# Transposes of 128 by 128 blocks in two row halves with 64 by 64 identities

## The chip, the cores and the metric

The kernel runs on one core of one Trainium2 chip. The metric is the device time of one execution in microseconds. TensorE multiplies matrices, VectorE and ScalarE work elementwise, GpSimd does small copies, and SyncE issues the DMAs.

## The reference

One layer of a hybrid decoder runs on 256 prompt tokens and 8 tokens of 8 sequences that are being decoded, 264 columns in all, everything in fp32:

```
h = rms_norm(x, g_pre_mix);  z = h @ w_in              # q, k, v, u
attn = sliding-window attention (window 128, 16 heads of 64, 2 kv heads, ALiBi, sinks)
ssm  = 64 groups of 16 channels, complex diagonal state of 64:
       s_t = ab * s_{t-1} + bb u_t ;  y = Re(C s) + D u ;  gelu ; per-group GLU
x += rms_norm([rms_norm(attn); rms_norm(ssm)] @ w_out)
x += rms_norm(SwiGLU(rms_norm(x)))                     # d_ff 5632
x += sigmoid(x @ w_ple_gate) * (p @ w_ple_proj)
```

The outputs are both x, the last 128 keys and values, and the last states.

## The kernel before

Activations lie transposed, with the model dimension on the 128 partitions and the 264 tokens as columns. The weights come from DRAM as 367 blocks of 512 KB in a fixed order (`UNITS`): `in`, `oa`, `os`, `pp`, `gu`, `dn`, `pg`. From the fifteenth block on each is split into a high and a low part, by ScalarE (`wh`) and VectorE (`wl`), and every 128 by 128 block makes three products of 264 columns into an accumulator `acc`: high with high, high with low, low with high.

The first stage does `in` and `oa`, and beside it all of the attention and of the state-space model. `os` needs the whole result of the latter, and from there on weight products follow one another to the end. Inside the first stage the state-space model runs in eight rounds e. `ssm_x` builds a table X on VectorE, transposes it on TensorE in eight blocks (tile `px`, line 968, copied to `XT`), makes `ph` in column tiles of 32, transposes that once (`ht`) and sends it through DRAM to get the table T. `ssm_w` multiplies the inputs with XT and T (`pw`, `py`), copies `pw` to `ws` and transposes it in four blocks (`pw2`, line 1049) to `wt`, on which VectorE runs the scan. `ssm_y` adds the state's part to `py` in 64 by 64 products (line 1112), applies GELU, transposes in four blocks (`py2`, line 1123) to `yt`, and stores that for `ssm_glu`, which loads it as `gt`. The attention runs in eight groups g; each transposes its probabilities in six blocks (`pt`, lines 586 to 589) to `ptt`, which the products `o` use. The profile names tiles without their numbers: `pw2` shows as pw and `py2` as py on line 289.

A transpose is one TensorE instruction, `PE.transpose(out, in_, ident)`: the block is the stationary operand, and a 128 by 128 identity moves through. Products whose operands lie on 64 of the 128 rows or go to 64 or 32 of the 128 columns are made in tiles of the array: `s` (64 rows), `o`, `pw` and `py` with T (64 columns), the state's part of `py` (64 by 64), `ph` (32 columns).

The program's order is not written out by hand. Each piece of work is a generator that names the engine it needs next and what it waits for; `Pace.run` keeps a modelled clock for each engine with a cost per instruction (`tr`: 0.11 us) and takes the piece that can start first, and by a priority among equals. Accumulator banks are counted there: 8 in all, 3 kept for weight products (`acc`, 2 after the tenth block) and the others (`bk`) for everything else; `"+bk:2"` asks for two. The scheduler under it places instructions once more in the first stage; from `os` on the order stays as written.

Of the kernel before, what the change touches and what calls it, by code (L numbers as in the profile page):

```python
# [16 lines left out]
P = 128  # L17
# [180 lines left out]
def build(nc, tc, ctx, a):  # L198
    pace = Pace()
    V, S, G, PE, SP = nc.vector, nc.scalar, nc.gpsimd, nc.tensor, nc.sync  # L200
# [86 lines left out]
    def tr(out, in_, ident):  # L287
        pace.use("pe", 0.11)
        PE.transpose(out, in_, ident)  # L289

    def dma(out, in_):
        n = 4.0
# [24 lines left out]
    def bank(shape, name):  # L317
        return banks.tile(shape, F32, tag="bank", name=name)
# [5 lines left out]
    ident = const.tile([P, P], F32, name="ident")  # L324
# [219 lines left out]
    def attn(g):  # L544

        yield "pe", [f"q{g}", "k", "v", "c_at"] + ([f"sfree{g - 1}"] if g else []) + ["+bk:2"]
        q = qt.pop(g)

        sh = [bank([P, 384], f"s{h}") for h in range(2)]
        for c, b, n in ((0, 0, 128), (128, 128, 256)):  # L550
            for h in range(2):
                r = slice(64 * h, 64 * h + 64)
                mm(sh[h][:, c:c + n], q[r, b:b + 128], kt[r, 0:n], 0.115 if n == 128 else 0.22)
        pace.rel("q")
        yield "dve"
        s = ph1.tile([P, 768], F32, tag="s", bufs=1, name="s")
        mx = ph1.tile([P, 4], F32, tag="mx", bufs=2, name="mx")
        nm = ph1.tile([P, 4], F32, tag="nm", bufs=2, name="nm")
        es = ph1.tile([P, 4], F32, tag="es", bufs=2, name="es")
        den = ph1.tile([P, 4], F32, tag="den", bufs=2, name="den")  # L560
        for i, (dst, src, dd) in enumerate((
                (s[:, 0:128], sh[0][:, 0:128], dist[:, 128:256]), (s[:, 128:256], sh[1][:, 0:128], dist[:, 128:256]),
                (s[:, 256:512], sh[0][:, 128:384], dist), (s[:, 512:768], sh[1][:, 128:384], dist))):
            pace.use("dve", 0.13 + 1.042e-3 * size(dst))
            V.tensor_tensor_reduce(out=dst, in0=src, in1=dd, scale=-slopes[(i % 2) * GRP + g],
                                   scalar=sinks[:, g, i:i + 1], op0=ALU.add, op1=ALU.max, accum_out=mx[:, i:i + 1])
        pace.rel("bk", 2)
        ts(nm, mx, -1.0, ALU.mult)
        sub(es, sinks[:, g, :], mx)
        yield "act"  # L570
        act(es, es, ACTF.Exp)
        offs = [(0, 128), (128, 256), (256, 512), (512, 768)]
        for i, (b, e) in enumerate(offs):
            act(s[:, b:e], s[:, b:e], ACTF.Exp, bias=nm[:, i:i + 1], accum_out=den[:, i:i + 1])
        yield "dve"
        add(den, den, es)
        pace.use("dve", 0.1)
        V.reciprocal(out=den, in_=den)
        yield "act"
        for i, (b, e) in enumerate(offs):  # L580
            act(s[:, b:e], s[:, b:e], scale=den[:, i:i + 1])
        yield "pe", "+bk:2"
        pts = []
        for h in range(2):
            pt = bank([P, 3, P], "pt")
            tr(pt[:, 0, :], s[:, 128 * h:128 * h + 128], ident)
            for b in range(2):
                o = 256 + 256 * h + 128 * b
                tr(pt[:, 1 + b, :], s[:, o:o + 128], ident)
            pts.append(pt)  # L590
        pace.sig(f"sfree{g}", "pe")
        yield "act", "+ptt"
        ptt = ph1.tile([P, 2, 3, P], F32, tag="ptt", bufs=1, name="ptt")
        for h in range(2):
            act(ptt[:, h], pts[h])
        pace.rel("bk", 2)
        yield "pe", "+bk"
        o = bank([P, 256], "o")
        for h in range(2):
            r = slice(64 * h, 64 * h + 64)  # L600
            mm(o[r, :], vnat[:, 0, r], ptt[:, h, 0:2, :], 0.24, stop=False)
        for h in range(2):
            r = slice(64 * h, 64 * h + 64)
            mm(o[r, 128:256], vnat[:, 1, r], ptt[:, h, 2, :], 0.14, start=False)
        pace.rel("ptt")
        yield "act", ["+sqa", "ah"]
        ah = AH["t"]
        sq = ph1.tile([P, 256], F32, tag="sqa", bufs=1, name="sqa")
        act(ah[:, g, 0:256], o, scale=gat[:, g:g + 1])
        act(sq, o, ACTF.Square)  # L610
        yield "dve"
        stt(ah[:, 8 + g, 0:256], o, gat[:, g:g + 1], r32(ah[:, g, 0:256]), ALU.mult, ALU.subtract)
        pace.rel("bk")
        pace.rel("sqa")
        if g == 0:
            pace.use("dve", 0.2)
            V.tensor_copy(out=ssq_a[:, 0:256], in_=sq)
        else:
            add(ssq_a[:, 0:256], ssq_a[:, 0:256], sq)
        pace.sig(f"at{g}", "dve")  # L620
# [329 lines left out]
    def ssm_x(e):  # L950
        yield "sp", ["+X", "+xt", "iss4"]
        xtab = ph1.tile([P, 512], F32, tag="xtab", name="xtab")
        dma(xtab, a["xtab"][e])
        b = xtab[:, 0:128].rearrange("p (r g c) -> p r g c", r=2, g=4)
        cb = xtab[:, 128:384].rearrange("p (r g c) -> p r g c", r=2, g=4)
        dp = xtab[:, 384:512]
        bs = ph1.tile([P, 4, 16], F32, tag="bs", name="bs")
        yield "pool"
        padd(bs, b[:, 0], b[:, 1])
        pcopy(cb[:, 1], cb[:, 1], -1.0)  # L960
        yield "dve", ["tab", "+sc"]
        X = ph1.tile([P, 2, 4, 8, 16], F32, tag="X", name="X")
        yield from outer(X, al_re, al2, b, bs, e)
        yield "pe", ["+bk:3", "+ht"] + ([f"Wpe{e - 1}"] if e else [])
        px = [bank([P, 4, P], f"px{i}") for i in range(2)]
        for g in range(4):
            for ri in range(2):
                tr(px[ri][:, g, :], X[:, ri, g].rearrange("p j c -> p (j c)"), ident)
        ph = bank([P, P], "ph")
        for g in range(4):  # L970
            for ri in range(2):
                PE.matmul(ph[32 * g:32 * g + 32, :], cb[:, ri, g, :], X[:, ri, g].rearrange("p j c -> p (j c)"),
                          start=(ri == 0), stop=(ri == 1), tile_position=(0, 32 * g))
                pace.use("pe", 0.11)
        pace.rel("X")
        yield "act"
        xt = ph1.tile([P, 4, 2, 2, 64], F32, tag="XT", bufs=1, name="XT")
        XT[e] = xt
        ht = ph1.tile([P, P], F32, tag="ht", name="ht")
        act(ht, ph)  # L980
        for ri in range(2):
            act(xt[:, :, :, ri, :], px[ri].rearrange("p g (h q) -> p g h q", h=2))
        pace.rel("bk", 3)
        pace.sig(f"XT{e}", "act")
        yield "pe", "+bk"
        p2 = bank([P, P], "p2")
        tr(p2, ht, ident)
        pace.rel("ht")
        yield "dve"
        t7 = ph1.tile([P, P], F32, tag="t7", name="t7")  # L990
        add(t7, p2, dp)
        pace.rel("bk")
        yield "sp", [f"U{e - NT2}"] if e >= NT2 else ["c_zero"]

        d = td[e % 2][:]
        dma(td[e % 2][0:P], t7)
        pace.rel("xt")
        yield "sp"
        dma(T2[e % NT2], bass.AP(tensor=d.tensor, offset=d.offset, ap=[[P, P], [16 * P, 8], [1, P]]))
        pace.sig(f"T{e}", "sp")  # L1000
# [14 lines left out]
    def ssm_w(e):  # L1015
        q, hf = e // 2, e % 2
# [3 lines left out]
        for h in range(2):  # L1020
            c = q + 4 * h
# [3 lines left out]
        xt = XT.pop(e)  # L1025
# [10 lines left out]
        for g in range(4):  # L1036
            for h in range(2):
                o = 16 * (2 * g + h)
                r = 64 * (h ^ (g % 2))
# [3 lines left out]
        ws = ph1.tile([P, 4, P], F32, tag="ws", bufs=1, name="ws")  # L1043
        act(ws, pw)
        pace.rel("bk")
        yield "pe", "+bk"
        p2 = bank([P, 4, P], "pw2")
        for g in range(4):
            tr(p2[:, g, :], ws[:, g, :], ident)
        pace.rel("ws")  # L1050
        yield "act", ["+wt", "as0"]
        wt = ph1.tile([P, 2, 4, 41], F32, tag="wt", name="wt")
        for h in range(2):
            for ri in range(2):
                act(wt[64 * h:64 * h + 64, ri], p2[64 * ri:64 * ri + 64, :, 64 * h:64 * h + 41])
        pace.rel("bk")
        yield "dve", [f"rho{e}", "rot2"]
        C2, S2 = ct[:, gsl(e), :].unsqueeze(1).to_broadcast([P, 2, 4, 32]), st2[:, :, gsl(e), :]
        t1, t2, sh = rt1, rt2, rsh
# [41 lines left out]
    def ssm_y(e):  # L1101
        q, hf = e // 2, e % 2
# [14 lines left out]
        for i in range(2):  # L1117
            act(gy[:, i::2, :], py[i], ACTF.Gelu_apprx_tanh)
        pace.rel("bk", 2)
        yield "pe", "+bk"  # L1120
        p2 = bank([P, 4, P], "py2")
        for g in range(4):
            tr(p2[:, g, :], gy[:, g, :], ident)
        pace.rel("ws")
        yield "act", "+yt"
        yt = ph1.tile([P, 4, P], F32, tag="yt", name="yt")
        act(yt[:, 0::2, :], p2[:, 0::2, :])
        act(yt[:, 1::2, :].rearrange("p g (h k) -> p g h k", h=2), p2[:, 1::2, :].rearrange("p g (h k) -> p g h k", h=2)[:, :, ::-1, :])
        pace.rel("bk")
        yield "sp"  # L1130
        dma(ys[q].rearrange("r c g h k -> (r c) g (h k)")[:, gs, :], yt)
        pace.sig(f"ys{q}{hf}", "sp")
# [610 lines left out]
```

## Time and profile before

| | |
|---|---|
| median of 3 runs | 1196.16 us (1195.06 to 1196.48) |
| profiled execution | 1194.09 us |
| its span, first to last instruction | 1192.3 us |
| TensorE products | 1172.4 us busy, 98% |
| VectorE | 744.7 us, 62% |
| ScalarE | 577.1 us, 48% |
| granted TensorE clock | 0.999 |

Products are pipelined, and the end of each in the profile is modelled: a product of 264 columns shows as 0.28 us though the next starts 0.12 us later. So distances between starts tell what an instruction costs, not its shown duration.

### The profile page before, as it was taken

The page shows a single profiled execution, that of the slowest core. Times are in us where ns is not written, and L with a number is a line of the kernel's source. Part 1 is how long each engine was busy: PE and PEld are TensorE (multiplying, and loading weights), DVE is VectorE, ACT ScalarE, POOL GpSimd, SP SyncE. Part 2 cuts the span into 40 slices and gives each one's busy share as a digit, 9 for nine tenths or more (in the row PEclk, how much of TensorE's full clock was granted, in tenths as well). Part 3 has the DMA queues.
Part 4 walks back from the last instruction along what each step waited for, and adds up shares of the span by engine and source line. Part 5 has one row for each costly group of instructions (what it writes and reads, how often), then busy time and mean ns, then how long its engine had stood idle before and what let it go on. Part 6 is the DMA issues. An engine that isn't in the chain of part 4 may idle for free.

```text
span 1192.3 us, 24043 instructions
## 1 busy us (share of the span) xinstructions
PE 1172.4 (98%) x9785; PEld 1142.1 (96%) x9785; DVE 744.7 (62%) x1316; ACT 577.1 (48%) x917; POOL 57.5 (5%) x96
## 2 busy tenths in 40 slices
PE   9999999989999999999999999999999999999998
PEld 7789888879999999999999999999999999999998
DVE  8888889857896555555555555555444444446864
ACT  6267886444655444444444444444333443345542
POOL 4113122100000000000000000000000000000000
PEclk9999999999999999999999999999999999999999
DMA  7866655656676565555555566556755555556683
GB/s 269 256 206 187 178 162 172 199 180 200 211 252 178 182 186 181 184 183 179 182 182 184 178 181 188 180 180 199 242 178 179 181 185 180 179 181 216 202 250 111
DMA packets 102053, 228.95 MB, mean 192 GB/s; under 512 B 26711, under 2 KB 50359, under 8 KB 101431
## 3 DMA queue, kind: packets, MB, share of 16 engines
q1 hardware_dynamic: 101943, 227.43, 60.7%
q8 instruction: 76, 1.25, 0.4%
q14 instruction: 34, 0.28, 0.1%
HBM read 214.60 MB, written 12.80 MB: 191 GB/s over the span
## 4 chain that ended last, share of the span: by engine, by line
PE 85%; DVE 8%; DMA 3%; ACT 2%; issue 1%; SPq 0%; POOL 0%; ACTq 0%; DVEq 0%; POOLq 0%
PE acc L285 80%; DVE wl L222 1%; PE py L285 1%; DMA T<-td 1%; DVE rt L222 1%; DMA pt<-in_p 1%; ACT s L281 1%; DMA xr<-in_x 0%; DVE xl L222 0%; DVE sc L222 0%; DVE ssq_x L222 0%; PE px L289 0%; DVE X L222 0%; SPq L296 0%; DMA gt<-ys 0%
## 5 line engine op out<-in xcount | busy, mean ns | idle before, releaser
L222 DVE TENSOR_TENSOR wl<-raw,wh 128x1024 fp32r<-128x1024 f32 x354 | 432.7, 1223 | 305.6 <-PE acc L285 278.7
L281 ACT ACTIVATE wh<-raw 128x1024 fp32r<-128x1024 f32 x354 | 375.5, 1061 | 439.5 <-PE acc L285 428.2
L285 PE MATMUL acc<-hh,wh 128*128 128x264 f32 x1408 | 399.5, 284 | 0.0
L285 PE MATMUL acc<-hl,wh 128*128 128x264 f32 x1408 | 398.3, 283 | 0.5 <-DVE hl L236 0.5
L285 PE MATMUL acc<-hh,wl 128*128 128x264 f32 x1408 | 398.6, 283 | 0.0
L285 PEld LDWEIGHTS acc<-hl,wh 128*128 128x128 f32 x1408 | 265.0, 188 | 0.8 <-DVE hl L236 0.7
L285 PEld LDWEIGHTS acc<-hh,wh 128*128 128x128 f32 x1408 | 265.2, 188 | 0.0
L285 PEld LDWEIGHTS acc<-hh,wl 128*128 128x128 f32 x1408 | 264.0, 188 | 0.0
L285 PE MATMUL acc<-f,wh 128*128 128x264 f32 x1408 | 256.8, 284 | 0.0
L285 PEld LDWEIGHTS acc<-f,wh 128*128 128x128 f32 x1408 | 217.8, 188 | 0.1
L285 PE MATMUL acc<-f,wl 128*128 128x264 f32 x704 | 199.7, 284 | 0.0
L285 PEld LDWEIGHTS acc<-f,wl 128*128 128x128 f32 x704 | 132.5, 188 | 0.0
L285 PE MATMUL acc<-x2h,wh 128*128 128x264 f32 x256 | 72.7, 285 | 0.0
L285 PE MATMUL acc<-x2h,wl 128*128 128x264 f32 x256 | 72.5, 284 | 0.0
L285 PE MATMUL acc<-x2l,wh 128*128 128x264 f32 x256 | 71.9, 284 | 0.2 <-DVE x2l L222 0.2
L285 PE MATMUL acc<-xh,wh 128*128 128x264 f32 x176 | 54.2, 308 | 0.0
L285 PE MATMUL acc<-xt,raw 128*128 128x264 f32 x224 | 52.1, 390 | 1.7 <-ACT xt L281 1.7
L285 PEld LDWEIGHTS acc<-xt,raw 128*128 128x128 f32 x224 | 42.3, 192 | 10.1 <-ACT xt L281 2.6
L222 DVE TENSOR_TENSOR uu<-acc,Rf 128x264 f32<-128x264 f32 x44 | 19.0, 432 | 51.0 <-PE acc L285 51.0
L285 PE MATMUL acc<-xh,wl 128*128 128x264 f32 x176 | 50.3, 286 | 0.0
L285 PE MATMUL acc<-xl,wh 128*128 128x264 f32 x176 | 50.1, 285 | 0.0
L285 PE MATMUL acc<-aops,wh 128*128 128x264 f32 x256 | 50.0, 293 | 0.0
(323 smaller groups left out, 1335.3 us busy)
## 6 DMA issues: line engine op xcount, KB each, us to landing
raw<-in_w SPq DMA_DIRECT2D x367, 512.0 KB, 3.6
T<-td SPq DMA_DIRECT2D x8, 512.0 KB, 4.8
xs<-in_x SPq DMA_DIRECT2D x2, 1056.0 KB, 6.9
ppd<-ppt SPq DMA_DIRECT2D x16, 132.0 KB, 3.6
x1d<-oo SPq DMA_DIRECT2D x4, 528.0 KB, 4.6
x<-x1d SPq DMA_DIRECT2D x2, 1056.0 KB, 8.9
ppr<-ppd SPq DMA_DIRECT2D x16, 132.0 KB, 3.9
xtab<-in_xtab SPq DMA_DIRECT2D x8, 256.0 KB, 3.4
```

Source lines behind the costliest of these rows:

```text
L222: V.tensor_tensor(out=out, in0=in0, in1=in1, op=op)
L281: S.activation(out=out, in_=in_, func=func, **kw)
L285: PE.matmul(out, lhsT, rhs, start=start, stop=stop)
```

## The change

A new helper `trh` makes a transpose in two instructions. Half h takes rows 64h to 64h+63 of the block as stationary operand (64 rows, 128 columns) and the 64 by 64 identity on the same rows as the moving one; its result is 64 columns wide. The two halves go to two different tiles, each in a bank of its own, so px and pt are divided between their two banks by row half instead of by part, and `pw2` and `py2` take two banks in place of one. The copies out of the banks follow: those of px and pt keep number and size, those of `wt` too, and `yt` is made in four copies of 128 columns in place of two of 256. Four places use it: the six transposes of `pt`, eight of `px`, four of `pw2`, four of `py2`. Those of `ht`, of v and of the decode tokens' attention stay. The planner's cost is 0.056 us for a half.

```diff
--- before.py
+++ after.py
@@ -287,6 +287,13 @@
     def tr(out, in_, ident):
         pace.use("pe", 0.11)
         PE.transpose(out, in_, ident)
+
+    def trh(outs, in_):
+
+        for h, out in enumerate(outs):
+            r = slice(64 * h, 64 * h + 64)
+            pace.use("pe", 0.056)
+            PE.transpose(out, in_[r], ident[r, r])
 
     def dma(out, in_):
         n = 4.0
@@ -580,19 +587,17 @@
         for i, (b, e) in enumerate(offs):
             act(s[:, b:e], s[:, b:e], scale=den[:, i:i + 1])
         yield "pe", "+bk:2"
-        pts = []
+        pts = [bank([P, 2, 3, 64], f"pt{i}") for i in range(2)]
         for h in range(2):
-            pt = bank([P, 3, P], "pt")
-            tr(pt[:, 0, :], s[:, 128 * h:128 * h + 128], ident)
+            trh([pt[:, h, 0, :] for pt in pts], s[:, 128 * h:128 * h + 128])
             for b in range(2):
                 o = 256 + 256 * h + 128 * b
-                tr(pt[:, 1 + b, :], s[:, o:o + 128], ident)
-            pts.append(pt)
+                trh([pt[:, h, 1 + b, :] for pt in pts], s[:, o:o + 128])
         pace.sig(f"sfree{g}", "pe")
         yield "act", "+ptt"
         ptt = ph1.tile([P, 2, 3, P], F32, tag="ptt", bufs=1, name="ptt")
-        for h in range(2):
-            act(ptt[:, h], pts[h])
+        for i in range(2):
+            act(ptt[:, :, :, 64 * i:64 * i + 64], pts[i])
         pace.rel("bk", 2)
         yield "pe", "+bk"
         o = bank([P, 256], "o")
@@ -965,7 +970,7 @@
         px = [bank([P, 4, P], f"px{i}") for i in range(2)]
         for g in range(4):
             for ri in range(2):
-                tr(px[ri][:, g, :], X[:, ri, g].rearrange("p j c -> p (j c)"), ident)
+                trh([px[h][:, g, 64 * ri:64 * ri + 64] for h in range(2)], X[:, ri, g].rearrange("p j c -> p (j c)"))
         ph = bank([P, P], "ph")
         for g in range(4):
             for ri in range(2):
@@ -978,8 +983,8 @@
         XT[e] = xt
         ht = ph1.tile([P, P], F32, tag="ht", name="ht")
         act(ht, ph)
-        for ri in range(2):
-            act(xt[:, :, :, ri, :], px[ri].rearrange("p g (h q) -> p g h q", h=2))
+        for h in range(2):
+            act(xt[:, :, h], px[h].rearrange("p g (r q) -> p g r q", r=2))
         pace.rel("bk", 3)
         pace.sig(f"XT{e}", "act")
         yield "pe", "+bk"
@@ -1043,17 +1048,17 @@
         ws = ph1.tile([P, 4, P], F32, tag="ws", bufs=1, name="ws")
         act(ws, pw)
         pace.rel("bk")
-        yield "pe", "+bk"
-        p2 = bank([P, 4, P], "pw2")
+        yield "pe", "+bk:2"
+        p2 = [bank([P, 4, 64], f"pw2{h}") for h in range(2)]
         for g in range(4):
-            tr(p2[:, g, :], ws[:, g, :], ident)
+            trh([p2[h][:, g, :] for h in range(2)], ws[:, g, :])
         pace.rel("ws")
         yield "act", ["+wt", "as0"]
         wt = ph1.tile([P, 2, 4, 41], F32, tag="wt", name="wt")
         for h in range(2):
             for ri in range(2):
-                act(wt[64 * h:64 * h + 64, ri], p2[64 * ri:64 * ri + 64, :, 64 * h:64 * h + 41])
-        pace.rel("bk")
+                act(wt[64 * h:64 * h + 64, ri], p2[h][64 * ri:64 * ri + 64, :, 0:41])
+        pace.rel("bk", 2)
         yield "dve", [f"rho{e}", "rot2"]
         C2, S2 = ct[:, gsl(e), :].unsqueeze(1).to_broadcast([P, 2, 4, 32]), st2[:, :, gsl(e), :]
         t1, t2, sh = rt1, rt2, rsh
@@ -1117,16 +1122,17 @@
         for i in range(2):
             act(gy[:, i::2, :], py[i], ACTF.Gelu_apprx_tanh)
         pace.rel("bk", 2)
-        yield "pe", "+bk"
-        p2 = bank([P, 4, P], "py2")
+        yield "pe", "+bk:2"
+        p2 = [bank([P, 4, 64], f"py2{h}") for h in range(2)]
         for g in range(4):
-            tr(p2[:, g, :], gy[:, g, :], ident)
+            trh([p2[h][:, g, :] for h in range(2)], gy[:, g, :])
         pace.rel("ws")
         yield "act", "+yt"
         yt = ph1.tile([P, 4, P], F32, tag="yt", name="yt")
-        act(yt[:, 0::2, :], p2[:, 0::2, :])
-        act(yt[:, 1::2, :].rearrange("p g (h k) -> p g h k", h=2), p2[:, 1::2, :].rearrange("p g (h k) -> p g h k", h=2)[:, :, ::-1, :])
-        pace.rel("bk")
+        for h in range(2):
+            for i in range(2):
+                act(yt[:, i::2, 64 * h:64 * h + 64], p2[h ^ i][:, i::2, :])
+        pace.rel("bk", 2)
         yield "sp"
         dma(ys[q].rearrange("r c g h k -> (r c) g (h k)")[:, gs, :], yt)
         pace.sig(f"ys{q}{hf}", "sp")
```

## Rows read from the trace of the kernel before

**Rows 1.** The page: busy time, share, instructions; and the chain that ended last.

```profile
PE 1172.4 (98%) x9785; PEld 1142.1 (96%) x9785; DVE 744.7 (62%) x1316; ACT 577.1 (48%) x917; POOL 57.5 (5%) x96
...
PE 85%; DVE 8%; DMA 3%; ACT 2%; issue 1%; SPq 0%; POOL 0%; ACTq 0%; DVEq 0%; POOLq 0%
```

**Rows 2.** Busy time by stretch: PE, PEld, DVE, ACT, POOL, clock, DMA share, GB/s.

```profile
200.00:220.00 20.00, 20.00 (x208) 18.72 (x207) 18.37 (x35) 10.60 (x22) 4.96 (x8) 1.00 0.71 194
...
240.00:260.00 20.00, 18.14 (x161) 16.88 (x158) 11.65 (x21) 8.22 (x14) 0.63 (x2) 1.00 0.58 167
260.00:280.00 20.00, 15.80 (x126) 15.37 (x126) 11.43 (x26) 9.42 (x15) 0.00 (x0) 1.00 0.57 202
```

**Rows 3.** Instructions of line 289 (transposes): ns min/median/max, starts, rows*columns.

```profile
L289 PEld LDWEIGHTS px<-ident,X x64: 137/140/143, 46.8 to 225.5; 128*128 128x128 f32 x64
L289 PE MATMUL px<-ident,X x64: 270/272/273, 47.1 to 225.6; 128*128 128x128 f32 x64
...
L289 PEld LDWEIGHTS ptd<-ident,pself x2: 83/84/86, 167.9 to 168.1; 128*8 128x8 f32 x2
```

**Rows 4.** Timeline of TensorE, 125.7 to 128 us: start, us from start, instruction, count.

```profile
125.75 0.82 PE L289 MATMUL pt<-ident,s 128*128 128x128 f32 x6
126.32 0.37 PE L285 MATMUL acc<-xh,wh 128*128 128x264 f32 x1
126.53 0.28 PE L285 MATMUL acc<-xl,wh 128*128 128x264 f32 x1
126.66 0.28 PE L285 MATMUL acc<-xh,wl 128*128 128x264 f32 x1
126.86 0.93 PE L285 MATMUL s<-kt,q 64*128 64x128 f32 x8
127.72 0.39 PE L285 MATMUL acc<-xh,wh 128*128 128x264 f32 x1
127.95 0.29 PE L285 MATMUL acc<-xl,wh 128*128 128x264 f32 x1
```

**Rows 5.** Chain of waits, 85 to 145 us: start, us on the chain, work, count.

```profile
89.56 0.44 PE pw L289 x4
...
97.99 1.03 PE py L285 x32
...
104.65 0.59 PE py L289 x4
...
106.72 0.87 PE px L289 x8
107.59 0.59 PE ph L972 x16
```

**Rows 6.** Timeline of TensorE, 163.9 to 164.4 us.

```profile
163.89 0.38 PE L289 MATMUL pt<-ident,s 128*128 128x128 f32 x2
164.03 0.37 PE L285 MATMUL acc<-xh,wh 128*128 128x264 f32 x1
164.24 0.38 PE L289 MATMUL pt<-ident,s 128*128 128x128 f32 x2
```

**Rows 7.** Timeline of TensorE, 61 to 62 us.

```profile
60.99 0.87 PE L289 MATMUL pt<-ident,s 128*128 128x128 f32 x6
61.79 0.93 PE L285 MATMUL s<-kt,q 64*128 64x128 f32 x8
```

**Rows 8.** Groups of ScalarE, 30 to 265 us: busy us, mean ns, idle before.

```profile
L281 ACT ACTIVATE yt<-py 128x256 f32<-128x256 f32 x16 | 5.3, 391 | 1.5 <-PE py L289 1.5
...
L281 ACT ACTIVATE ht<-ph 128x128 f32<-128x128 f32 x8 | 2.2, 272 | 0.0
```

**Rows 9.** Chain of waits from 225 us (two rows), and TensorE's timeline at the end of the stage.

```profile
231.35 6.30 DMA T<-td
...
253.86 4.18 DMA gt<-ys
...
263.54 0.69 PE L285 MATMUL ps_s<-ssq_s,onesh 128*128 128x264 f32 x2 [3.35 <-DVE ssq_s L222]
```

## The prediction

> **What bounds the kernel now.** I read the page first, then its chain of waits, the table by stretches, and for the stages with transposes the timeline of TensorE and the groups of line 289. TensorE is busy 98% of the span and carries 85% of the chain that ended last [rows 1]. All converted transposes lie between 46 and 250 us, in the first stage. Up to 240 us TensorE has hardly a hole: 20.00 of 20.00 us in 200 to 220, 18.14 in 240 to 260, and 15.80 in 260 to 280 [rows 2]. From about 264 us it runs weight products to the end, and nothing there changes. So the question is when the first stage lets `os` begin. Before 225 us that is mostly a matter of TensorE's own length; after it a chain of waits decides: a 6.30 us round trip through DRAM for T, 4.18 us for `gt`, and TensorE stands 3.35 us before the norm that opens `os` [rows 9].
>
> **What is removed and added.** 176 transposes go: 8 groups of 8 (px), 8 of 6 (pt), 8 of 4 (pw2) and 8 of 4 (py2). Each becomes two halves with 64 rows, 128 stationary columns and 64 moving ones. The 17 others (ht, v, decode) stay.
>
> *Price of a transpose now.* A px group of eight takes 0.87 us on the chain, a pw2 group of four 0.44 [rows 5]: 0.109 us each, for 128 moving columns. Half the columns are 0.055 us by proportion. Its weight load must fit behind that: for transposes a load of 128 columns takes 140 ns and one of 8 columns 84 [rows 3], so 120 columns cost 56 ns and 128 about 60.
>
> *Do the halves run side by side?* No half transpose is in the trace, so I bound a pair. The nearest rows are products on 64 rows. The s group has four instructions of 128 columns and four of 256; one after another they would take 4 x 0.109 + 4 x 0.218 = 1.31 us, and they take 0.86 from the first to the next product, 126.86 to 127.72 [rows 4]. The 64 by 64 products of py, 32 of 128 columns, would take 3.5 us and take 1.03 [rows 5]. So tiles overlap, and the best case of a pair is 0.055, the worst (one half after the other, or no load behind a running half) 0.109. I take 0.057, nearer to the rows that overlap. Saved: 176 x (0.109 - 0.057) = 9.2 us of TensorE time; bounds 0 and 9.5.
>
> *What the change of tile size costs.* This is the term that eats the gain. Full-size products start 0.12 us apart (126.53, 126.66). From the last of them to s there are 0.20, so 0.08 to 0.09 are lost; behind s the first two start at 127.72 and 127.95, 0.23 apart, so 0.11 are lost again, besides 0.09 before them [rows 4]. For a transpose the entry is seen directly: four cost 0.44 behind full-size work and 0.59 behind `o`, which uses half the columns [rows 5]: 0.15 for the entry. The exit is 0.09 + 0.11 = 0.20. Today pt to products costs nearly none of this (126.32 to 126.53 is 0.21, but the first stands only 0.03 behind the last transpose, so 0.01 is lost) [rows 4]. A full excursion is then 0.15 + 0.20 - 0.01 = 0.34 us.
>
> *How many excursions.* I counted the neighbours of each group on the timeline of TensorE.
> The 8 px groups stand between products and ph, which is a tile of its own and pays its entry already (0.59 for work that overlaps four ways) [rows 5]; they add an entry only, 8 x 0.15 = 1.2 us.
> Five pt groups stand alone between products, as at 125.75 [rows 4]; two are cut into three pieces by single products, as at 163.89 [rows 6], which makes five full excursions and one exit. Seven pw2 and five py2 groups stand alone, one py2 is cut in two. That is 5 + 5 + 7 + 5 + 2 = 24 full excursions, 8.2 us.
> Three stand behind work in tiles and add an exit, 0.6 us. One pt stands before an s [rows 7], which will have its tile size: a switch less, 0.2 us saved. One py2 stands behind an s, and I price it at nothing.
> Sum 1.2 + 8.2 + 0.6 - 0.2 = 9.8 us against 9.2 saved: TensorE is 0.6 us longer in all. By kind: a px group gains 0.27, a pt group loses 0.03, a group of four loses 0.13.
>
> *The copies.* px and pt keep count and size of their ScalarE copies; both pt copies now need all six transposes where the first needed three, at most 3 x 0.109 = 0.33 us later, behind which only `o` of the same group waits, with products to fill TensorE. wt keeps its four. yt goes from two copies of 256 to four of 128: 391 and 272 ns [rows 8], so between 0 and 4 x 0.272 - 2 x 0.391 = 0.31 us more; I take 0.15, since copies overlap a little. It is on the path once, in the last round.
>
> *The banks.* pw2 and py2 hold two accumulator banks where they held one. If each group had to wait for one more copy, it would be 16 x 0.39 [rows 8] = 6.2 us; if the banks are free, nothing. I take nothing, since products, for which banks are held already, fill such a wait. No DMA, no VectorE instruction and no order by hand is changed; but the planner sees two banks asked for and 0.112 for a transpose instead of 0.11, so the order can move by itself.
>
> *The path.* Up to the last px, at about 225 us, TensorE is some 0.5 us longer, of which little is caught by holes. In the tail px ends 0.27 earlier, pw2 and py2 hand over 4 x 0.052 - 0.15 = 0.06 earlier each, yt 0.15 later: -0.2. Net +0.3 us. The profiled execution took 1194.1 us (span 1192.3), so 1194.4; the median of the runs is 2.1 us above it, so **1196.5 us**.
>
> The Trainium skill speaks against my 0.057 in one place: "TensorE: Matmul & The Clock Gate", Part 3 on packing small matmuls, says that a weight load overlaps a running matmul only where the row group differs. By that rule a pair on the same two row groups would be about 0.055 + 0.060 = 0.115 us, and the sum would be +10.9 instead of +0.6. The trace disagrees for full-size work: products on all rows start 0.12 apart, and only behind a switch does their load show, with 0.11 more [rows 4].
>
> **Rivals.**
> *Halves don't overlap (slower).* A pair costs 0.109 (one half after the other) to 0.115 (its load of 0.060 before its 0.055), nothing is saved, and the excursions remain: +9.8 to +10.9 us of TensorE, of which holes of the stage take 1 to 2. For it: no half transpose is in the trace, and a transpose might not be split as a product is. Against: s and py [rows 4, 5]. About 1205 us; it decides once a pair is over 0.07 (176 x 0.013 = 2.3). This is also what that rule of the skill's page would give.
> *The order breaks up (slower).* Products already cut pt groups in pieces [rows 6]; every further cut costs 0.34 and was free before. If the eight pt groups are all cut in three and the sixteen groups of four in two, these are some 27 more: +9; a third of that, with some waits for banks, is +3 to +4, about 1200 us. For it: two of eight are cut now. Against: groups of four mostly come whole.
> *The loop of rounds is the bound (faster).* Each round hands px to pw2 to py2 and through DRAM to the next. If that loop and not TensorE's length sets the end, the exits cost nothing, since only filler stands behind them, and eight rounds gain 0.27 + 0.06 + 0.06 each: -3.1, less 0.15: 1193.2 us. For it: the tail from 225 us is such a chain [rows 9]. Against: 20.00 of 20.00 us in 200 to 220 [rows 2]. Luck of the order gives similar sizes.
> *The change does nothing* can be left out as its own case: it gives the forecast's time.
>
> **How the numbers follow.** About 0.2% (2.4 us) is what a measurement of this kernel can tell from no change. Chances: the break-even forecast 0.47; halves without overlap 0.12; a broken order or banks 0.19; the loop or a lucky order 0.22. The first gives "same" alone (0.47); the second and third give slower, 0.31; the fourth faster, 0.22. The range for 8 in 10 takes in the loop, with some luck of order beneath it, and the broken order, and cuts most of the case without overlap: 1191.5 to 1204.0. The forecast's own range is 1194.5 to 1198.5.
>
> **What would show it.** Pairs of px: the group of 16 in about 0.46 us of starts besides its entry; if it takes 0.87 the first rival holds. Products behind pt, pw2 and py2: first start 0.09 late and the next 0.23 apart. TensorE's holes before 240 us no larger than now, the last px near 225 us, `os` beginning near 264 us, yt in four copies. If the count of groups cut by products has grown, the order broke; if `os` begins 2 us or more earlier with TensorE as full as now, the loop was the bound. I would be wrong above all through the price of a pair, the one term with no row of its own, or through an order that I can't see.

## The result

The changed kernel takes 1214.55 us (1212.57 to 1215.92), against 1196.32 for the kernel before: 1.0150 times, with a 95% interval of 1.0130 to 1.0169. I had forecast 1196.5 and a range up to 1204.0. The loss is 18 us, and no rival of mine names its mechanism at that size.

The price of the halves is close to what I worked out. The timeline of TensorE in the changed kernel shows one lone pt group, one pw2 group, and one px group with its ph:

```profile
108.98 0.28 PE L285 MATMUL acc<-xh,wl 128*128 128x264 f32 x1
109.19 0.59 PE L296 MATMUL pt<-ident,s 64*128 64x64 f32 x12
109.71 0.39 PE L285 MATMUL acc<-xh,wh 128*128 128x264 f32 x1
109.94 0.28 PE L285 MATMUL acc<-xl,wh 128*128 128x264 f32 x1
...
114.31 0.28 PE L285 MATMUL acc<-xh,wl 128*128 128x264 f32 x1
114.52 0.46 PE L296 MATMUL pw<-ident,ws 64*128 64x64 f32 x8
114.91 0.39 PE L285 MATMUL acc<-xh,wh 128*128 128x264 f32 x1
115.14 0.28 PE L285 MATMUL acc<-xl,wh 128*128 128x264 f32 x1
...
117.81 0.28 PE L285 MATMUL acc<-xh,wl 128*128 128x264 f32 x1
118.02 0.71 PE L296 MATMUL px<-ident,X 64*128 64x64 f32 x16
118.66 0.66 PE L977 MATMUL ph<-X,xtab 128*32 128x128 f32 x16
```

Read starts, and take off 0.12 for each full-size product between them. The pt group with entry and exit costs 109.94 - 108.98 - 0.24 = 0.72 us, against 0.66 before (125.75 to 126.53, less 0.12) [rows 4]: 0.06 more, where I had 0.03. The pw2 group costs 115.14 - 114.31 - 0.24 = 0.59 against 0.44 [rows 5]: 0.15 more, where I had 0.13. px up to ph costs 118.66 - 117.81 - 0.12 = 0.73; before, the same stretch (130.53 to 131.61, less 0.12, in the rows below) took 0.96: 0.23 less, where I had 0.27. From the spans between groups of 8, 12 and 16, a further pair costs (118.66 - 118.02 - 114.91 + 114.52) / 4 = 0.0625 us; I had taken 0.057. Over 8 px, 8 pt and 16 groups of four this makes about +1 us.

```profile
130.53 0.28 PE L285 MATMUL acc<-xh,wl 128*128 128x264 f32 x1
130.65 1.03 PE L289 MATMUL px<-ident,X 128*128 128x128 f32 x8
131.61 0.67 PE L972 MATMUL ph<-X,xtab 128*32 128x128 f32 x16
```

What moved is the order. The px instructions of the changed kernel, in the columns of rows 3 (ns, then the first and the last start in us):

```profile
L296 PE MATMUL px<-ident,X x128: 221/223/274, 47.8 to 247.1; 64*128 64x64 f32 x128
```

And TensorE's largest waits in the changed kernel from 60 to 290 us (us in total, times, longest):

```profile
PE py L285 <- DMA T<-td: 7.5, 4, 3.3
PE zb L285 <- DMA gt<-ys: 5.6, 1, 5.6
PE py L285 <- DVE SB L222: 3.2, 1, 3.2
PE o L285 <- ACT ptt L281: 2.6, 3, 2.1
PE ps_s L285 <- DVE ssq_s L222: 2.5, 1, 2.5
```

The same in the kernel before:

```profile
PE ps_s L285 <- DVE ssq_s L222: 3.4, 1, 3.4
PE py L285 <- DMA T<-td: 3.2, 3, 1.4
PE py L285 <- DVE SB L222: 1.1, 2, 0.9
PE zb L285 <- DMA gt<-ys: 1.0, 1, 1.0
```

The first px stands where it stood, the last one ends its starts at 247.1 instead of 225.6 [rows 3]. The second px already comes at 94.67; before it came at 73.8. So one round is 21 us late, some of that is made up by the next (118.02 against 106.56, 11 us late), and the last rounds lose it again. TensorE waited 3.2 us for T in the kernel before, 1.0 for `gt` and 1.1 for SB; here 7.5, 5.6 and 3.2. With the wait for ptt (2.6), that of the norm before `os` (2.5) and two smaller ones (0.9 and 0.8), the waits up to `os` add up to 23.1 us; before they were 10.0.

The table by stretches answers to rows 2; first the kernel before in 80 to 100 us, then the changed one:

```profile
80.00:100.00 20.00, 19.77 (x199) 18.80 (x198) 16.26 (x35) 11.41 (x24) 4.41 (x7) 1.00 0.76 217
...
80.00:100.00 20.00, 19.05 (x205) 16.98 (x204) 11.93 (x33) 11.18 (x25) 1.32 (x2) 1.00 0.60 174
...
260.00:280.00 20.00, 10.67 (x84) 9.06 (x81) 6.98 (x15) 5.41 (x14) 0.63 (x2) 0.69 0.39 102
```

From 80 to 100 us TensorE looks full, but it is full of attention and weight products: VectorE, which has the tables of the late round to make, is busy 11.93 us there against 16.26 before. At 260 to 280 us the bill comes. The weight products of `oa` are used up, the last round is still on its way, TensorE is busy 10.67 of 20 us, and after its waits the granted clock is 0.69, a mix of the full 2.4 and the half 1.2 GHz. `os` begins at 283.6 us instead of 263.9:

```profile
263.99 0.28 PE L285 MATMUL acc<-aops,wl 128*128 128x264 f32 x1
267.51 2.42 PE L285 MATMUL py<-G,SB 64*64 64x128 f32 x32 [3.23 <-DVE SB L222]
...
276.89 1.22 PE L285 MATMUL zb<-gt,wg 128*128 128x264 f32 x2 [5.59 <-DMA gt<-ys]
...
283.56 0.60 PE L285 MATMUL acc<-sops,wh 128*128 128x264 f32 x2
```

That is 19.7 of the 21.5 us between the two profiled spans (1213.8 and 1192.3 us); from `os` to the end the two kernels take 930.2 and 928.4 us.

### The profile page after: what moved, and what is told of

Same layout as the page of the kernel before. It is cut to its first block, busy times and chain, and to the rows that moved or that the text cites. A ratio compares the mean times of both kernels' runs of the same rounds, so it can differ in the third digit from the quotient of the medians.

```text
span 1213.8 us, 24408 instructions
## 1 busy us (share of the span) xinstructions
PE 1179.2 (97%) x9961; PEld 1142.8 (94%) x9961; DVE 745.7 (61%) x1316; ACT 578.1 (48%) x932; POOL 45.7 (4%) x96
## 4 chain that ended last, share of the span: by engine, by line
PE 85%; DVE 7%; DMA 5%; ACT 2%; issue 1%; SPq 0%; ACTq 0%; DVEq 0%
PE acc L285 80%; DMA T<-td 2%; PE py L285 1%; DMA td<-t 1%; DVE wl L222 1%; DMA pt<-in_p 1%; DVE rt L222 1%; DMA xr<-in_x 0%; DVE s L572 0%; DVE ssq_x L222 0%; DVE xl L222 0%; ACT s L281 0%; PE o L285 0%; SPq L303 0%; DVE G L222 0%
```

## The experiments

Two theories stood against each other. **Order:** the halves cost next to nothing, and the planner, which now sees two banks asked for and other costs, puts the rounds in a worse order. **Tiles:** the switches of tile size cost more than the trace before let me see.

**Half transposes in the old order, full ones in the new order.** Each kernel gets the other's planner inputs; the two orders of pieces are then those of the kernel before and of the changed one.

```
# halves_order_before: the changed kernel, but
-            pace.use("pe", 0.056)
+            pace.use("pe", 0.055)
-        yield "pe", "+bk:2"        # at pw2 and py2; both banks are still taken
+        yield "pe", "+bk"
...
+        pace.use("act", -0.18)     # yt
-        pace.rel("bk", 2)
+        pace.rel("bk")
# full_order_after: the kernel before, but
-        pace.use("pe", 0.11)       # tr, for px, pt, pw2, py2
+        pace.use("pe", 0.112)
-        yield "pe", "+bk"          # at pw2 and py2; one bank is taken
+        yield "pe", "+bk:2"
...
+        pace.use("act", 0.18)      # yt
```

> Half transposes in all four places, with their two banks and four yt copies, placed in the order of the kernel before: the planner is told of one bank, 0.055 us a half and the old time for yt. Theory 'order': 1195 to 1199 us, as the sum of the prediction (+0.3) has it, with perhaps a wait for the ninth bank. Rival 'tiles': as slow as the changed kernel, 1210 to 1217 us.

> Full transposes as in the kernel before, placed in the order of the changed kernel: the planner is told of two banks for pw2 and py2 (one is taken), 0.112 us for a transpose and 0.18 us more for the copies of yt, so that its order is that of the changed kernel, piece by piece. Theory 'order' (the two banks asked for make the planner put the second round's px behind two attention groups, and all later rounds with it): 1212 to 1217 us, second px near 94 us, os from about 283 us. Rival 'tiles' (the switches between full-size products and half transposes cost the time): no half transpose is left, so 1195 to 1198 us.

| instructions | order of the kernel before | order of the changed kernel |
|---|---|---|
| full transposes | 1 | 1.0143 (1.0125 to 1.0161), 1212.32 us |
| half transposes | 1.0006 (0.9996 to 1.0015), 1195.88 us | 1.0150 (1.0130 to 1.0169), 1214.55 us |

In the traces the sequence of TensorE's instructions up to `os`, a pair counted as one, agrees to 99.4% between the two runs of the left column and to 99.6% between those of the right one; between the kernel before and the changed one it agrees to 65%. So the order makes the difference, and within either order the intervals don't tell the halves from the full transposes. The px instructions of the run with halves in the old order:

```profile
L296 PE MATMUL px<-ident,X x128: 221/222/275, 47.1 to 230.3; 64*128 64x64 f32 x128
```

And of the run with full transposes in the new order:

```profile
L289 PE MATMUL px<-ident,X x64: 270/273/273, 47.3 to 243.8; 128*128 128x128 f32 x64
```

The last start of px follows the order too: 230.3 near the 225.6 of before, 243.8 near the 247.1 of the changed kernel, and `os` begins at 267.7 and 279.3 us. "Tiles" is refuted: all its halves are in the run of 1195.88 us.

**px and pt alone.** Four edits of the change fall away (pw2, py2, their banks, yt).

> Only px and pt in halves (112 of 176 transposes); pw2 and py2 as before, so no bank more is asked for. Theory 'order': the planner's order hardly moves; the prediction's sum by kind gives 8 x (-0.27) + 8 x 0.03 and the cut groups, so 1194 to 1197 us. Rival 'tiles': about two thirds of the loss, 1205 to 1211 us.

1.0015 (1.0005 to 1.0024), 1196.77 us: far from the rival's 1205, but at the upper edge of what I expected, and slower by a little where the sum said faster. px starts from 46.9 to 226.8, so the order held nearly. Why it is slower I did not find; the run with px alone, further down, is some 4 us faster than this one.

**Which planner input?** Each of the next four leaves every instruction of the kernel before as it was and changes what the planner is told.

```
# claim_both: banks only             # costs_only: costs only
-  yield "pe", "+bk"                 -  pace.use("pe", 0.11)
+  yield "pe", "+bk:2"               +  pace.use("pe", 0.112)  # px, pt, pw2, py2
-  pace.rel("bk")                    ...
+  pace.rel("bk", 2)                 +  pace.use("act", 0.18)  # yt
# yt_cost_only: the last line alone   # tr_cost_only: the 0.112 alone
```

> The kernel before, every instruction of it, with one thing told to the planner: pw2 and py2 claim two banks (one is taken); all planner's costs as before. Theory 'banks' (the claim alone keeps the second px waiting and the loss follows from that): as slow as the changed kernel, 1210 to 1216 us, second px near 95 us. Rival 'order at large' (the planner's order is thrown by any small difference, and the loss is that of the one order which came out): second px near 95 us too, but the rounds behind it fall in another order and the time is anywhere, I take 1202 to 1209 us.

> The kernel before, every instruction of it, one bank for pw2 and py2 as before, and only the planner's costs of the changed kernel (0.112 us for a transpose of px, pt, pw2, py2; 0.18 us more for the copies of yt). Theory 'banks': no bank more is asked for, so 1194 to 1198 us. Rival 'order at large': second px near 74 us as before, but the rounds from the fourth on fall as late as in the changed kernel, and 1207 to 1215 us.

> The kernel before, every instruction of it, with one planner's cost changed: 0.18 us more for the copies of yt. If the loss of the run with all planner's costs comes from this one cost, 1208 to 1214 us. If the order is thrown only by the two costs together, the rounds fall somewhere else: I take 1195 to 1203 us.

> The kernel before, every instruction of it, with the other planner's cost changed: 0.112 us instead of 0.11 for a transpose of px, pt, pw2 and py2. If the loss comes from this cost, 1208 to 1214 us. If only from the two together, 1194 to 1199 us, since the run with px and pt in halves, which had this cost for most of them, kept the order.

| told to the planner | ratio | second px | last px ends its starts |
|---|---|---|---|
| two banks (claim_both) | 1.0104 (1.0087 to 1.0121) | 97.7 us | 240.5 us |
| both costs (costs_only) | 1.0140 (1.0125 to 1.0155) | 73.8 us | 244.4 us |
| yt 0.18 us dearer | 1.0050 (1.0036 to 1.0064) | as before | 230.5 us |
| transposes 0.002 us dearer | 1.0006 (0.9996 to 1.0017) | as before | 226.4 us |

The banks theory, as I had put it, is wrong: with one bank and only the costs changed the kernel loses as much as the changed one, by another way. Its second and third px come on time, its fourth at 138.82 instead of 130.65, as its timeline of TensorE shows (x6, since the window ends inside the group of eight):

```profile
138.82 0.82 PE L289 MATMUL px<-ident,X 128*128 128x128 f32 x6
```

The two costs together do more than the sum of each alone (1.4% against 0.5% and 0.06%), and banks and costs together no more than costs (1.5%). The run with the banks alone (1208.61 us) and those with one cost alone (1202.47 and 1196.57) lie where "order at large" and "only the two together" had them. The largest waits of TensorE in the run with both costs are near those of the changed kernel, though no instruction differs from the kernel before:

```profile
PE py L285 <- DMA T<-td: 8.3, 5, 2.8
PE zb L285 <- DMA gt<-ys: 5.6, 1, 5.6
PE py L285 <- DVE SB L222: 3.8, 2, 3.4
PE ps_s L285 <- DVE ssq_s L222: 2.4, 1, 2.4
```

**Giving the banks back earlier.** In the planner the copies of the first pw2 wait for the table as0, so that its two banks are held meanwhile and px, which asks for three at once, finds too few. The wait can stand one step later:

```
-        yield "act", ["+wt", "as0"]
+        yield "act", ["+wt"]
...
-        yield "dve", [f"rho{e}", "rot2"]
+        yield "dve", [f"rho{e}", "rot2", "as0"]
```

> The changed kernel, where the copies of pw2 to wt no longer wait for the table as0 (the VectorE step behind them waits for it), so that the first round's pw2 gives back its two banks some 20 us earlier. Theory 'order', in its narrow form (the two banks held by the first pw2 keep the second px waiting): second px back near 70 us, and most of the loss gone, 1197 to 1205 us. In its wide form (later rounds lose banks too): second px early, but 1206 to 1213 us. Rival 'tiles': 1213 to 1217 us.

1.0135 (1.0120 to 1.0150), 1212.18 us. The second px does come early, at 68.26 on the timeline of TensorE (its other halves at 69.38, behind a wait of 0.85 us for the copies to wt), so the held banks were what kept it:

```profile
68.26 0.27 PE L296 MATMUL px<-ident,X 64*128 64x64 f32 x1
```

But the last one is late all the same, as the px instructions of this run show:

```profile
L296 PE MATMUL px<-ident,X x128: 221/223/273, 47.1 to 238.8; 64*128 64x64 f32 x128
```

The narrow form falls and the wide one holds (1206 to 1213 us): the one late round isn't the loss, since later rounds fall badly without it.

**All halves but pw2, and the same order with full transposes.**

> Half transposes in px, pt and py2 (with its two banks and four yt copies); only pw2 as before. Theory 'banks': the bank that the first pw2 holds is the harm, that of py2 is held briefly, so 1195 to 1199 us. Rival 'order at large': the planner packs the rounds from the third on more closely, last px some 10 us earlier than before (near 214 us), and 1183 to 1192 us.

> Full transposes in the order of the run that has halves in all places but pw2 (planner told 0.112 us for px, pt and py2, two banks for py2, 0.18 us more for yt). Rival 'order at large': within 2 us of that run, whichever side of the kernel before it falls. If halves were worth something by themselves (shorter px on the path of each round), it is 2 to 4 us slower than that run.

1.0002 (0.9993 to 1.0011), 1196.22 us, and 1.0029 (1.0017 to 1.0041), 1199.66 us. The first has the time of theory 'banks' and the early px of "order at large", whose time I had wrong: its px are done at 216.2, nine us early, and the kernel is no faster. Its timeline of TensorE shows what ended last:

```profile
260.00 0.61 PE L285 MATMUL ps_s<-ssq_s,onesh 128*128 128x264 f32 x2
...
265.17 0.41 PE L285 MATMUL acc<-aops,wh 128*128 128x264 f32 x2
```

The norm that opens `os` runs at 260.00 without a wait, 3.5 us earlier than before, but TensorE still has products of `oa` to do until 265.5. The rounds were early and TensorE was not: it had stood idle in earlier stretches, 5.8 us of it waiting for T.

The pair differs by 0.27%, some 3 us, in nearly the same order (99.8% of the sequence), where in the order of the kernel before halves and full transposes can't be told apart. What the halves give of it isn't shown: `os` begins 3.7 us apart in the two traces, and the run with full transposes also has 6.4 us of TensorE's work at half the clock up to there, the other 3.4.

**px alone, and px with the banks given back earlier.**

> Only px in halves, the one kind for which the prediction's sum gives a gain: 8 x (-0.27) = -2.2 us of TensorE, planner's order as before. If a gain of TensorE reaches the end: 1193 to 1195 us, ratio near 0.998. If the stage's chain and not TensorE's length decides, or the order swallows it: 1195 to 1197 us, ratio 1.000.

> Only px in halves, and the copies of pw2 to wt no longer wait for the table as0, so that the first pw2 gives its bank back earlier and the second px can come earlier, at about 67 us. If banks held early were the bound of the kernel before: 1188 to 1193 us. If the order only falls differently: 1193 to 1200 us, on either side of the kernel before.

0.9977 (0.9968 to 0.9986), 1192.77 us: a gain of 2.7 us where the sum said 2.2. That it is the gain of the shorter px isn't shown. In the profiled execution `os` begins at 264.2 us, no earlier than before, and TensorE stands idle 2.3 us more up to there, so that the holes took what px saved; that execution was the slowest of its eleven, and the others have no trace. The order isn't quite that of the kernel before either (97.8% of the sequence), and pt, pw2 and py2 weren't run alone. With the earlier release 0.9950 (0.9938 to 0.9962), 1190.28 us, faster than both kernels. Its px instructions:

```profile
L296 PE MATMUL px<-ident,X x128: 221/222/274, 47.5 to 222.7; 64*128 64x64 f32 x128
```

The second of its px groups on the timeline of TensorE:

```profile
67.19 0.71 PE L296 MATMUL px<-ident,X 64*128 64x64 f32 x16
```

The earlier release without halves was not run, so how the 5.7 us divide between px, the release and a good throw of the order is open.

**All orders side by side.** From the start of `os` to the end the fourteen traces take 927 to 933 us; what parts the orders comes before it. In the five that lose 1% or more (the changed kernel, full_order_after, claim_both, costs_only, after_as0) TensorE stands idle 23.8 to 28.5 us before `os` begins, in the other nine 12.6 to 16.6.

## Why the prediction was wrong

*Halves run side by side, a pair about 0.057 us.* Right: 0.0625. Side by side with this, "TensorE: Matmul & The Clock Gate" of the Trainium skill, Part 3, would not let the load of the next pair run behind the present one on the same row groups; that would make 0.115 by the prediction's estimate, and this trace, with 0.0625, disagrees.

*A switch of tile size costs 0.34 us both ways.* Right in size: +0.06, +0.15 and -0.23 us per pt group, group of four and px group, where I had +0.03, +0.13 and -0.27. "TensorEngine Tiling (Array Packing)" of the Trainium skill, Key Properties, says that changing the tiling mode drains TensorE; the 0.21 us from the last product to pt (108.98 to 109.19) and the 0.23 between the first two behind it, against 0.12 elsewhere, fit that, though the trace doesn't show the drain itself.

*Net +0.3 us on the path, order as before.* Right for that order: the run that has it is at +0.06% with an interval from -0.04% to +0.15%, that is -0.5 to +1.8 us.

*"The planner sees two banks asked for and 0.112 for a transpose instead of 0.11, so the order can move by itself."* This is the step that failed. I saw that it could, took nothing for it, and bounded the banks by one ScalarE copy per group, 6.2 us. Measured, the new order alone, with full transposes, costs 1.43%, about 17 us. A bank that is held doesn't cost a copy: in the changed kernel it keeps the second px, which needs three banks at once, behind attention groups, 21 us late. But that one delay isn't the loss. With it taken away the kernel still takes 1212.18 us, and two small costs without any bank make 1212.73 us with the second px on time. What the five orders that lose 1% or more share is the end: the last product of `oa` starts 11 to 20 us before `os` does (7 us in the kernel before), since the last round is not done.

*The rival of a broken order.* Near, but by another mechanism: I priced cuts of groups by products, at +3 to +4. In the trace of the changed kernel no group is cut: px, pt, pw2 and py2 stand in 8 pieces each, where before pt stood in 12 and py2 in 9. It is the rounds that are displaced. The rival in which halves don't overlap had the right direction and is refuted. The loop of rounds as the bound was my rival for a gain; the waits that grew (T, SB, `gt`) are those of that loop, in the other direction.

*Where the loss sits.* TensorE's waits from 60 us to `os` are 13.1 us longer (23.1 against 10.0). It also works at half the clock in three stretches, which begin 0.0 to 1.5 us after a wait of TensorE has ended (2.1 us for ptt, 2.8 for T, 3.2 for SB); the kernel before has no such stretch up to there:

```profile
175.40:178.80 3.40, 3.40 (x24) 2.95 (x21) 2.50 (x6) 2.08 (x10) 0.62 (x2) 0.50 0.86 277
206.10:209.50 3.40, 3.40 (x22) 3.05 (x21) 1.57 (x2) 2.26 (x5) 0.00 (x0) 0.50 0.43 101
267.60:281.20 13.60, 7.05 (x48) 4.89 (x48) 1.74 (x6) 2.94 (x10) 0.45 (x2) 0.50 0.34 86
```

It is busy 13.85 us in them, and products start 0.22 us apart there (208.78, 209.00) instead of 0.12, so some 6 us are lost (an estimate). With 1 us for the halves that is about 20 us, all of the 19.7 by which `os` begins later.

What stays open: why one order of rounds leaves TensorE with more holes than another. The px of one run were done nine us earlier without a gain, so the place of px alone doesn't tell.

## What to carry to other kernels

Where a planner in the program makes the order from costs and counted buffers, a change has two parts, its instructions and its new order, and the second can be far larger: the orders run here lie from 0.5% under to 1.5% above the kernel before, and one new order is one draw from them. Run them apart: the new instructions with the old planner inputs, and the old instructions with the new ones. And when one edit asks for one buffer more, look for who needs several at once and what holds them longest, not for the length of one copy.

## What the hardware showed that I had not expected

After the waits at the end of the late stage the same work runs far slower: the 32 products of py, 1.03 us on the chain before [rows 5], take 2.46 in the changed kernel, and the first zb takes 1.22 instead of 0.68; from 267.6 to 281.2 us the granted clock is 0.50. The chain of waits of the changed kernel:

```profile
266.95 0.42 DVE SB L222
267.51 2.46 PE py L285 x32
270.00 0.39 ACT gy L281
270.43 0.90 PE py L296 x8
271.33 0.78 ACT yt L281 x4
272.13 2.01 DMA ys<-yt
274.16 0.37 SPq L303
274.58 2.17 DMA gt<-ys
276.89 1.22 PE zb L285 x2
```

py had stood 3.23 us before these products, waiting for SB, and zb 5.59 us. So these holes cost their length and then, at 1.2 instead of 2.4 GHz, some of the work behind them: 1.4 us for py alone, more than halving the clock gives (2 x 1.03 would be 2.06 us, not 2.46). Not every hole does: TensorE stood 3.35 us before the norm in the kernel before [rows 9], and the clock stayed at 1.00 [rows 2]. What decides I did not find. The load of `gt` in this chain is shorter than before (2.17 us against 4.18 [rows 9]); what is missing is products to fill TensorE meanwhile.
